# A transformer block's matrix products: high parts first, low parts last, with a new order in the opening and in the up stage

## The chip, the cores and the metric

The kernel runs on one core of a Trainium2 chip. The metric is the device time of one execution in microseconds (us). Three executions of the kernel before took 2151.69, 2151.9 and 2154.22 us; the median is 2151.9. Besides TensorE (PE), the core has VectorE (DVE), ScalarE (ACT), GpSimd (POOL) and SyncE (SP); the last one here issues most transfers.

## The reference

One residual block on a sequence of 2048 tokens of 1024 channels, float32:

```python
h = rmsnorm(x, norm_mix_pre)
u_pool, u_glu, g_a, g_b = split(h @ w_in)          # 512, 1024, 1024, 1024 columns
branch_a = pool_mixer(u_pool, ...)                 # trailing means, group maps, projection
branch_b = conformer_conv(u_glu, ...)              # GLU, causal conv of width 31, LayerNorm, swish, projection
merged = sigmoid(g_a) * branch_a + sigmoid(g_b) * branch_b
x = x + rmsnorm(merged @ w_o, norm_mix_post)
h = rmsnorm(x, norm_mlp_pre)
f = square(relu(h @ w_up)) @ w_down                # 1024 -> 4096 -> 1024
x = x + rmsnorm(f, norm_mlp_post)
```

## The kernel before

**Parts.** Every factor is kept as a high part in the type fp32r (`wh` of a weight, `big` or `tr` of a cell; a cast on ACT, line 237 for weights and 230 in the opening) and a low part (`wl`, or `big` and `tr` again; the rest, a subtraction on DVE at line 131). A product adds three of the four partial products: high by high, weight's high by cell's low, weight's low by cell's high.

**Products.** The large matrix products are cut in blocks of 1024 by 1024 tokens or channels and computed by schemes that need seven block products for eight (`Octet`, with its numbered products 1 to 7, `sink` receiving the finished blocks). Such a block product works on two cells of two 128-row pieces each (k = 0 to 3) and two output halves (q = 0, 1): 2 x 4 x 3 = 24 matmuls of 128x128 by 128x512. `product()` (line 301) issues them with `matmuls()` (line 276) for one half after the other, in the order of `passes()` (line 271): for each k high by high and then weight's high by cell's low, and the weight's low part last, just ahead of the last k. So a cell's low part is used from the second matmul on, the second cell's from the sixth, the weight's low part from the seventh. `in_order()` (line 312) issues them by a table of (q, k, weight part, cell part) and can call a function ahead of the n-th (`inside`). While the kernel is in its opening, `product()` uses the table STAIRS (line 59): cell by cell high by high, cell's low, weight's low, each for both halves.

**Stages.** The program runs, for two batches of 1024 tokens, the input projection (glu, pool, ga, gb), branch A, the merge with branch B (`B`), the output projection, and the up and down stages. The up stage of the first batch, 8 octets (`mlp_up(0, parts)`, line 1897), runs while the second batch's convolution is still to be done on DVE: 31 steps for each of four channel groups (lines 1066 and 1070), and then its norm over the channels (`norm_steps`, whose last parts are at lines 1133 to 1143). These steps are handed out by a lane with a rate, the number of steps per product; `conv1.rate` is 1.2 (line 1854), and `faster()` sets it to 2.8 after a given product of the second octet (`then(faster, octs[1])`, line 1898). Then B of the second batch begins. The norm ends for each of the four pieces so: load of the convolution `yd` to `tr`, times the factor `r` (DVE), sigmoid and gain (ACT), product of the two (DVE), store to `zd`, load of `zd` to `big`, cast at line 1205 (ACT), low part (DVE). B's matmuls take these `big` cells.

**What sets the order.** Every engine works through its own queue in the order of the program as a scheduler has laid it out; an instruction under `tc.high_priority(offset=URGENT)` is put further ahead. SP's queue holds loads and stores in one order, and an entry that waits holds back those behind it. In the up stage `sink` (line 1568) adds a held partial sum to the finished sum in PSUM (`mark(add(o, ps, s))`, line 1571, DVE line 128), which frees the PSUM buffer for a later product.

**The opening.** Lines 1690 to 1757 write out by hand the first eight block products (the glu's) with the loading, norming and splitting of the tokens' cells: `first_gain` (a gain on ACT), `first_cell` (line 924, times the norm factor on DVE), `cells0` (the split), `parts.need` (differences of cells), `n1.spread()` (the norm factor of the second 512 tokens, by eight small matmuls, and its copy to `r` on ACT).

Of the kernel before, what the change touches and what calls it, by code (L numbers as in the profile page):

```python
# [32 lines left out]
URGENT = 1500  # L33
# [22 lines left out]
START = ((0, 1), (0, 2), (1, 2), (1, 1), (0, 5), (0, 6), (0, 3), (0, 7))  # L56
START += ((1, 6), (0, 4), (1, 5), (1, 7), (1, 3), (1, 4))
ORDER = (1, 2, 6, 5, 7, 3, 4)
STAIRS = tuple(
    (q, 2 * c + k, wp, xp)  # L60
    for c in (0, 1) for wp, xp in ((0, 0), (0, 1), (1, 0)) for q in (0, 1) for k in (0, 1)
)
COMING = tuple((q, k, 0, 0) for k in (0, 1) for q in (0, 1)) + ((0, 0, 0, 1), (1, 0, 0, 1))
COMING += ((0, 2, 0, 0), (1, 2, 0, 0), (0, 0, 1, 0), (0, 1, 1, 0), (0, 2, 1, 0), (0, 3, 0, 0))
COMING += ((1, 3, 0, 0), (0, 3, 1, 0), (0, 1, 0, 1), (1, 1, 0, 1)) + tuple((1, k, 1, 0) for k in range(4))
# [11 lines left out]
def block_kernel(  # L77
# [14 lines left out]
    nc = tc.nc  # L92
# [34 lines left out]
    def add(o, a, b):  # L127
        return nc.vector.tensor_tensor(o, a, b, op=ALU.add)  # L128
# [21 lines left out]
    def mark(i):  # L150
        marks[i.ins.engine] = i.ins
        return i
# [145 lines left out]
            tuple(part[:, c * T : (c + 1) * T] for part in cell) for cell in cells for c in (0, 1)  # L298
        ]

    def product(ps, w, cells, start=True, stop=True):

        if in_opening:
            in_order(STAIRS, ps, w, cells, start, stop)
            return
        rhs = cell_rhs(cells)
        i = [matmuls(half_of(ps, q), w, 4 * q, rhs, start, stop) for q in (0, 1)]
        mark(i[1])

    in_opening = [True]  # L310

    def in_order(order, ps, w, cells, start, stop, inside=(None, None)):

# [147 lines left out]
    class Octet:  # L461
# [16 lines left out]
        def prepare(self, i):  # L478
            self.w[i] = self.weight(i)

        def run(self, i, then, bg):
            w, cells = self.w.pop(i, None) or self.weight(i), self.parts.need(i)
            if then is not None:
                self.parts.need(then)
            acc = {1: "x", 2: "z", 6: "x", 5: "y", 7: "x", 3: "y", 4: "x"}[i]
            begins = i in (1, 5) or (i == 2 and not self.seeded)
            if begins:
                self.ps[acc] = psum(self.lab)
            ps = self.ps[acc]
            product(ps, w, cells, start=begins, stop=i in (2, 3, 4))  # L490
            flush()
            if i == 1 and self.seeded:
                self.ps["z"] = psum(self.lab)
                mark(nc.scalar.copy(self.ps["z"], ps))
            elif i == 2 and self.seeded:
                self.sink(0, 0, ps, None)
            elif i == 1:
                self.s1 = self.held(ps)
                if self.s2 is not None:
                    self.sink(0, 0, self.s2, self.s1)  # L500
            elif i == 2 and self.s1 is None:
                self.s2 = self.held(ps)
            elif i == 2:
                self.sink(0, 0, ps, self.s1)
            elif i == 6:
# [13 lines left out]
    class Plain:  # L519
# [57 lines left out]
        def run(self, job, then, bg, inside=(None, None)):  # L577
            m, t, k = job
            w = self.w.pop(job, None) or self.weight(*job)
            cells = self.parts.need(self.part(job))  # L580
            if then is not None:
                self.parts.need(then)
            if k == 0:
                self.ps = psum(self.lab)
            if t == 0:
                order = COMING if (m, k) == (0, 0) else STAIRS
                in_order(order, self.ps, w, cells, k == 0, k == 1, inside)
            else:
                product(self.ps, w, cells, start=k == 0, stop=k == 1)
            flush()  # L590
            bg()
            if k and t:
                self.sink(m, t, self.ps, None)
            elif k:
                self.block[m] = tr()
                mark(nc.scalar.copy(self.block[m], self.ps))
# [326 lines left out]

    def first_cell(c, t):
        x = x0[c, t]
        if t or c > 1:
            first_gain(c, t)
            mul(two(x), two(x), per_token(r0[t]))
            return x
        for i in (0, 1):  # L930
            s = slice(i * T, (i + 1) * T)
            nc.vector.scalar_tensor_tensor(
                x[:, s], x[:, s], col(C_PRE + 2 * c + i), r0[t], op0=ALU.mult, op1=ALU.mult
            )
        return x
# [618 lines left out]
    def mlp_up(b, parts):  # L1554
        def one(u):
            f, other = {}, {}
            late = (b and u >= 2) or u >= 4

            def fetch_other():
                h = u - SLABS  # L1560
                for k, at in (
                    (("T3", (1, h, (0, 0))), ("T2", (1, h, "T1")), ("T4", (0, u, (0, 0))))
                    if u >= SLABS else (("T1", (0, u, (0, 0))),)
                ):
                    other[k] = fo()
                    load(other[k], fd[at])

            def sink(m, t, ps, s):
                o = tr()
                if s is not None:  # L1570
                    mark(add(o, ps, s))
                    ps = o
                mark(nc.scalar.activation(o, ps, AF.Relu))
                nc.scalar.activation(o, o, AF.Square)
                f[m, t] = o

                def keep(i, cell, how=load):
# [12 lines left out]
                if len(f) == 3 and (1, 0) not in f:  # L1590
                    d = tr()
                    sub(d, f[1, 1], f[0, 1])
                    keep("t3", d)
                    if late:
                        sub(f[0, 1], f[0, 1], f[0, 0])
                        keep("t1", f[0, 1])
                    if late:
                        e = f["e"] = tr()
                        add(e, d, f[0, 0])
                        keep("t2", e)  # L1600
                if late and (m, t) == (1, 0):
# [71 lines left out]
    def opening():  # L1673
# [50 lines left out]
        with tc.high_priority(offset=URGENT):  # L1724
            cells0(2, 0)
            n1.root()
            cells0(3, 0)
            parts.step()
            o2.prepare(2)
            first_gain(0, 1)  # L1730
            parts.need(2)
            first_gain(1, 1)
        fix()
        o2.run(1, None, none)
        with tc.high_priority(offset=URGENT):
            n1.spread()
            o1.prepare(0, 1, 0)
            o1.get(1)
            cells0(0, 1), cells0(1, 1)
            first_gain(2, 1)  # L1740
            parts.need(8)
            first_gain(3, 1)
        fix()
        o2.run(2, None, none)
        with tc.high_priority(offset=URGENT):
            o1.prepare(0, 1, 1)
            cells0(2, 1), cells0(3, 1)
            parts.need(3)
            o1.cast_behind = [
                i for i in nc.cur_bb.bb.instructions if i.engine == mybir.EngineType.Activation  # L1750
            ][-1]
        fix()
        o1.load_behind = fix.last[E.SP]
        dve.last.update(fix.last)
        in_opening.clear()

    opening()
    with behind():
# [136 lines left out]
        conv1.rate = 2.8  # L1895

    octs = mlp_up(0, parts)
    then(faster, octs[1])
    run(octs, soon=3)
    empty()  # L1900
    early.close()
# [569 lines left out]
    for n, (s, i, b) in enumerate(END):  # L2471
        if n == 0:
            acc[0, b] = psum("down")
        end.append(coming.pop(0))
        product(acc[0, b], weight_down(i, s, 0), end[n], start=n == 0, stop=s == LAST)
        if n + 2 < SLABS:
            coming.append(token_cells(*END[n + 2]))
        w = [weight_down(i, n, 1, BIG)] if n == 0 else w + [weight_down(i, n, 1, BIG)]
        if s == LAST:
            last_product(i, 0, b, acc[0, b])  # L2480
        bg()
# [75 lines left out]
```

## Time and profile before

| | |
|---|---|
| median of three executions | 2151.9 us |
| the profiled execution | 2153.48 us |
| its span in the profile | 2151.7 us |
| matmuls on PE | 9549 |
| DVE instructions, busy | 1621, 1653.8 us |
| mean clock granted to PE | 0.997 of full |

The span runs from the first to the last instruction that the profiler recorded; the execution's own time holds 1.78 us more around it. In the rows below, a line gives the start in us, the busy time, the engine, the source line, the operation with its output and inputs, and in brackets how long the engine stood idle before it and which instruction's end released it.

### The profile page before, as it was taken

How to read it: one execution, taken by the hardware profiler on the slowest of the kernel's cores; microseconds unless marked ns; L12 is line 12 of the kernel's file. 1: busy time of each engine (PE TensorE's matmuls, PEld its weight loads, DVE VectorE, ACT ScalarE, POOL GpSimd, SP SyncE). 2: the span in 40 equal slices, each digit the busy share in tenths (PEclk: the TensorE clock that was granted, in tenths of full speed). 3: DMA queues.
4: the chain of work that ended last, by engine and by line, in shares of the span. 5: the costliest groups of instructions: out<-in, count | busy, mean ns of one | idle time of the engine just before them, and what ended most of it. 6: DMA issues, size and time to landing. Idle time of an engine off the chain costs nothing.

```text
span 2151.7 us, 25228 instructions
## 1 busy us (share of the span) xinstructions
PE 2130.3 (99%) x9549; PEld 1764.8 (82%) x9549; DVE 1653.8 (77%) x1621; ACT 1047.7 (49%) x1123; POOL 78.4 (4%) x143
## 2 busy tenths in 40 slices
PE   9999999999999999999999999999999999999998
PEld 7888888888888887888888888888888888888887
DVE  7898589997778869997868795667776657576975
ACT  8445454334443635445554684645663332234751
POOL 1000000000000000000000000000000000120002
PEclk9999999999999999999999999999999999999999
DMA  8789897768897787445697698677898997996977
GB/s 309 250 301 344 310 354 263 270 246 304 338 362 251 267 320 270 169 148 200 248 352 296 244 347 319 249 262 277 316 347 313 346 379 258 336 366 236 302 260 209
DMA packets 174506, 620.49 MB, mean 288 GB/s; under 512 B 19504, under 2 KB 21808, under 8 KB 174384
## 3 DMA queue, kind: packets, MB, share of 16 engines
q1 hardware_dynamic: 143456, 508.01, 64.8%
q0 software_dynamic: 17824, 64.07, 8.4%
q10 hardware_dynamic: 13104, 46.80, 5.5%
q8 instruction: 75, 1.23, 0.2%
q14 instruction: 47, 0.39, 0.0%
HBM read 408.99 MB, written 209.81 MB: 288 GB/s over the span
## 4 chain that ended last, share of the span: by engine, by line
PE 90%; DVE 5%; DMA 3%; ACT 1%; issue 1%; SPq 0%; DVEq 0%; ACTq 0%
PE up L280 24%; PE down L280 22%; PE wo L280 8%; PE ga L280 7%; PE gb L280 7%; PE glu L280 5%; PE rb L280 5%; PE A L280 4%; PE B L280 4%; PE pool L280 3%; DVE y L1070 1%; DVE big L131 1%; DVE tr L131 1%; PE glu L319 1%; DVE wl L131 1%
## 5 line engine op out<-in xcount | busy, mean ns | idle before, releaser
L280 PE MATMUL up<-big,wh 128*128 128x512 f32 x1792 | 481.3, 390 | 5.0 <-DVE tr L128 4.2
L280 PEld LDWEIGHTS up<-big,wh 128*128 128x128 f32 x1792 | 336.4, 188 | 76.2 <-issue 3.9
L237 ACT CAST wh<-wr 128x1024 fp32r<-128x1024 f32 x196 | 205.8, 1051 | 336.2 <-PE up L280 101.8
L1070 DVE SCALAR_TENSOR_TENSOR y<-v,cst,y 128x1024 f32<-128x1024 f32 x240 | 307.5, 1281 | 3.1
L280 PE MATMUL down<-big,wh 128*128 128x512 f32 x872 | 294.9, 389 | 0.0
L237 ACT CAST wh<-ws 128x1024 fp32r<-128x1024 f32 x128 | 134.6, 1052 | 302.3 <-PE up L280 91.6
L280 PE MATMUL up<-big,wl 128*128 128x512 f32 x896 | 277.0, 390 | 0.0
L280 PE MATMUL down<-big,wl 128*128 128x512 f32 x688 | 212.0, 389 | 0.0
L131 DVE TENSOR_TENSOR wl<-ws,wh 128x1024 fp32r<-128x1024 f32 x120 | 146.5, 1221 | 76.1 <-ACT wh L237 75.6
L280 PEld LDWEIGHTS up<-big,wl 128*128 128x128 f32 x896 | 168.7, 188 | 35.0
L280 PE MATMUL down<-tr,wh 128*128 128x512 f32 x504 | 196.2, 389 | 0.5 <-DVE tr L131 0.5
L280 PEld LDWEIGHTS down<-big,wh 128*128 128x128 f32 x872 | 163.6, 188 | 33.9
L131 DVE TENSOR_TENSOR wl<-wr,wh 128x1024 fp32r<-128x1024 f32 (+1 forms) x121 | 146.3, 1211 | 32.3 <-ACT wh L237 32.3
L131 DVE TENSOR_TENSOR big<-big,big 128x1024 fp32r<-128x1024 f32 (+1 forms) x108 | 129.9, 1221 | 41.0 <-ACT big L1205 19.6
L131 DVE TENSOR_TENSOR tr<-tr,big 128x1024 fp32r<-128x1024 f32 x94 | 112.6, 1221 | 56.5 <-ACT big L1975 43.8
L280 PEld LDWEIGHTS down<-big,wl 128*128 128x128 f32 x688 | 129.1, 188 | 26.8
L280 PE MATMUL wo<-big,wh 128*128 128x512 f32 x480 | 128.5, 389 | 0.0
L1975 ACT CAST big<-tr 128x1024 fp32r<-128x1024 f32 x70 | 72.0, 1048 | 102.1 <-DMA tr<-fd 79.9
L280 PE MATMUL gb<-big,wh 128*128 128x512 f32 x448 | 120.1, 389 | 0.0
L280 PE MATMUL ga<-big,wh 128*128 128x512 f32 x448 | 119.8, 389 | 0.0
L280 PEld LDWEIGHTS down<-tr,wh 128*128 128x128 f32 x504 | 94.6, 188 | 20.5 <-DVE tr L131 1.0
L280 PEld LDWEIGHTS wo<-big,wh 128*128 128x128 f32 x480 | 90.0, 188 | 18.5
(248 smaller groups left out, 3427.0 us busy)
## 6 DMA issues: line engine op xcount, KB each, us to landing
tr<-fd SPq DMA_DIRECT2D x98, 512.0 KB, 7.5
wl<-kept SPq DMA_DIRECT2D x85, 512.0 KB, 4.9
wr<-w_down SPq DMA_DIRECT2D x80, 512.0 KB, 7.5
kept<-wl SPq DMA_DIRECT2D x72, 512.0 KB, 6.2
wr<-w_up SPq DMA_DIRECT2D x64, 512.0 KB, 5.3
wr<-w_in SPq DMA_DIRECT2D x59, 512.0 KB, 5.2
fd<-tr ACTq DMA_DIRECT2D x54, 512.0 KB, 5.4
big<-fd SPq DMA_DIRECT2D x48, 512.0 KB, 6.4
```

The source lines that it names most:

```text
L131: return nc.vector.tensor_tensor(o, a, b, op=ALU.subtract)
L237: nc.scalar.copy(hi[:, :n], src[:, :n])
L280: i = nc.tensor.matmul(ps, w[wp][:, (at + k) * P : (at + k + 1) * P], rhs[k][xp], start=start and n == 0, stop=stop and n == len(order) - ...
L319: i = nc.tensor.matmul(half_of(ps, q), w[wp][:, (4 * q + k) * P : (4 * q + k + 1) * P], rhs[k][xp], start=start and q not in seen, stop=st ...
L1070: nc.vector.scalar_tensor_tensor(acc, v[:, k : k + TB], wk, acc, op0=ALU.mult, op1=ALU.add)
L1975: nc.scalar.copy(hi, t)
```

## The change

It has four parts. First, `product()` takes a table: by default LATE_LOWS, which runs the high by high matmuls of both cells first, then the first cell's low part, the weight's low part with both cells, and the second cell's low part last. A cell's low part is used from the 9th matmul on (the first cell's) or from the 21st (the second's), the weight's low part from the 13th. The products at the end of the down stage keep the old order (None); branch A, the merge and the output projection don't go through `product()`. Second, in the opening the fifth and sixth product (`o2.run(1, ...)` and `o2.run(2, ...)`) use STAIRS and issue the work for the second 512 tokens after 20 of their 24 matmuls; cell (3, 1) is normed and gained by two DVE instructions rather than by ACT and DVE; the seventh and eighth product use LOWS_BEHIND. Third, the additions in the up stage's `sink` are put ahead. Fourth, `faster()` is called after a product of the third octet rather than of the second.

```diff
+def cellwise(*steps):
+    return tuple(
+        (q, 2 * c + k, wp, xp) for c, wp, xp in steps for q in (0, 1) for k in (0, 1)
+    )
+STAIRS = cellwise(*((c, *part) for c in (0, 1) for part in ((0, 0), (0, 1), (1, 0))))
+LOWS_BEHIND = cellwise(*((c, *part) for c in (0, 1) for part in ((0, 0), (1, 0), (0, 1))))
+LATE_LOWS = cellwise((0, 0, 0), (1, 0, 0), (0, 0, 1), (0, 1, 0), (1, 1, 0), (1, 0, 1))
...
-    def product(ps, w, cells, start=True, stop=True):
-        if in_opening:
-            in_order(STAIRS, ps, w, cells, start, stop)
+    def product(ps, w, cells, start=True, stop=True, order=LATE_LOWS):
+        if order is not None:
+            in_order(order, ps, w, cells, start, stop)
             return
...
-            product(ps, w, cells, start=begins, stop=i in (2, 3, 4))
+            if inside is not None:
+                in_order(STAIRS, ps, w, cells, begins, i in (2, 3, 4), inside)
+            else:
+                product(ps, w, cells, start=begins, stop=i in (2, 3, 4))
...
-                product(self.ps, w, cells, start=k == 0, stop=k == 1)
+                product(self.ps, w, cells, k == 0, k == 1, LATE_LOWS if m else LOWS_BEHIND)
...
-        if t or c > 1:
+        if (c, t) not in ((0, 0), (1, 0), (3, 1)):
             first_gain(c, t)
             mul(two(x), two(x), per_token(r0[t]))
             return x
...
-                    mark(add(o, ps, s))
+                    with tc.high_priority(offset=URGENT):
+                        mark(add(o, ps, s))
...
-            first_gain(1, 1)
         fix()
-        o2.run(1, None, none)
-        with tc.high_priority(offset=URGENT):
-            n1.spread()
-            o1.prepare(0, 1, 0)
-            o1.get(1)
-            cells0(0, 1), cells0(1, 1)
-            first_gain(2, 1)
-            parts.need(8)
-            first_gain(3, 1)
+        def second_half():
+            with tc.high_priority(offset=URGENT):
+                n1.spread()
+                first_gain(1, 1)
+                o1.prepare(0, 1, 0)
+                o1.get(1)
+                cells0(0, 1), cells0(1, 1)
+                parts.need(8)
+                first_gain(2, 1)
+        def last_cells():
+            with tc.high_priority(offset=URGENT):
+                o1.prepare(0, 1, 1)
+                cells0(2, 1), cells0(3, 1)
+                parts.need(3)
...
+        o2.run(1, None, none, (20, second_half))
         fix()
-        o2.run(2, None, none)
...
+        o2.run(2, None, none, (20, last_cells))
...
-    then(faster, octs[1])
+    then(faster, octs[2])
...
-        product(acc[0, b], weight_down(i, s, 0), end[n], start=n == 0, stop=s == LAST)
+        product(acc[0, b], weight_down(i, s, 0), end[n], n == 0, s == LAST, None)
```

What that moves in the queues is seen in rows of the compiled programs. A row gives the source line, the operation, the output and inputs (tiles with running numbers, which differ by a little between the two programs) and the size. Lines of the changed program are 7 or 8 higher.

The first place is on DVE in the opening, from the norming of the second 512 tokens' last cells on (`big_376` and `big_378` are cells (2, 1) and (3, 1), `r_213` the norm factor). Before:

```order
L134 TENSOR_TENSOR big_372<-big_372,r_213 128x1024
L134 TENSOR_TENSOR big_374<-big_374,r_213 128x1024
L131 TENSOR_TENSOR big_586<-big_372,big_585 128x1024
L131 TENSOR_TENSOR big_590<-big_374,big_589 128x1024
L128 TENSOR_TENSOR tr_621<-glu_595,tr_563 128x1024
L134 TENSOR_TENSOR big_376<-big_376,r_213 128x1024
L134 TENSOR_TENSOR big_378<-big_378,r_213 128x1024
L131 TENSOR_TENSOR tr_648<-big_372,big_217 128x1024
L131 TENSOR_TENSOR big_631<-big_376,big_630 128x1024
L131 TENSOR_TENSOR big_635<-big_378,big_634 128x1024
```
After:

```order
L141 TENSOR_TENSOR big_372<-big_372,r_213 128x1024
L141 TENSOR_TENSOR big_374<-big_374,r_213 128x1024
L138 TENSOR_TENSOR big_578<-big_372,big_577 128x1024
L138 TENSOR_TENSOR big_582<-big_374,big_581 128x1024
L141 TENSOR_TENSOR big_376<-big_376,r_213 128x1024
L940 SCALAR_TENSOR_TENSOR big_378<-big_378,cst,r_213 128x512 x2
L138 TENSOR_TENSOR big_622<-big_376,big_621 128x1024
L138 TENSOR_TENSOR big_626<-big_378,big_625 128x1024
L135 TENSOR_TENSOR tr_634<-glu_593,tr_591 128x1024
L138 TENSOR_TENSOR tr_647<-big_372,big_217 128x1024
L138 TENSOR_TENSOR tr_653<-big_374,big_219 128x1024
```
The cells (2, 1) and (3, 1) now come ahead of the addition `tr_634<-glu_593,...`, their low parts too, and (3, 1) is made by two instructions of line 940.

The second place is on DVE in the first up stage, near the end of an octet (`tr_6615<-up_6287` before and `tr_6614<-up_6286` after are the addition in `sink`; `wl_6672` and `wl_6671` are the low part of a next product's weight, `big_6580` and `big_6586` low parts of cells). Before:

```order
L131 TENSOR_TENSOR tr_6577<-big_5448,tr_6199 128x1024
L1070 SCALAR_TENSOR_TENSOR y_6353<-v_5618,cst,y_6353 128x1024
L131 TENSOR_TENSOR tr_6583<-big_5526,tr_6243 128x1024
L131 TENSOR_TENSOR wl_6672<-wr_6435,wh_6671 128x1024
L131 TENSOR_TENSOR big_6580<-tr_6577,big_6579 128x1024
L131 TENSOR_TENSOR big_6586<-tr_6583,big_6585 128x1024
L128 TENSOR_TENSOR tr_6615<-up_6287,tr_6476 128x1024
L1070 SCALAR_TENSOR_TENSOR y_6353<-v_5618,cst,y_6353 128x1024
```
After:

```order
L138 TENSOR_TENSOR tr_6576<-big_5447,tr_6198 128x1024
L1078 SCALAR_TENSOR_TENSOR y_6352<-v_5617,cst,y_6352 128x1024
L138 TENSOR_TENSOR tr_6582<-big_5525,tr_6242 128x1024
L135 TENSOR_TENSOR tr_6614<-up_6286,tr_6475 128x1024
L138 TENSOR_TENSOR big_6579<-tr_6576,big_6578 128x1024
L138 TENSOR_TENSOR big_6585<-tr_6582,big_6584 128x1024
L138 TENSOR_TENSOR wl_6671<-wr_6434,wh_6670 128x1024
L138 TENSOR_TENSOR tr_6620<-tr_6614,tr_6560 128x1024
L1078 SCALAR_TENSOR_TENSOR y_6352<-v_5617,cst,y_6352 128x1024
```
The addition now stands ahead of the two cells' low parts and the weight's.

The third place is on SP at the end of the first up stage, where the four pieces of the second batch's convolution are loaded (`yd`), stored normed (`zd`) and loaded again, among loads of weights (`wr`, `wl`), stores of the up stage's results (`fd`) and loads for B's merge (`sbd`, `mad`). Before, from the load of the fourth piece:

```order
L137 DMA tr_8370<-yd_168 128x1024
L137 DMA zd_173<-tr_8244 128x1024
L137 DMA zd_174<-tr_8283 128x1024
L137 DMA big_8578<-zd_173 128x1024
L137 DMA zd_175<-tr_8325 128x1024
L137 DMA big_8581<-zd_174 128x1024
L137 DMA zd_176<-tr_8370 128x1024
L137 DMA big_8584<-zd_175 128x1024
L137 DMA wr_8831<-w_co 128x1024
L137 DMA wl_8612<-kept_4937 128x1024
L137 DMA big_8587<-zd_176 128x1024
```
After, from the store that stands ahead of the load of the fourth piece (this program's last rows of the four `zd` stand further down, at the load `big_8586<-zd_176`):

```order
L144 DMA zd_173<-tr_8385 128x1024
L144 DMA wr_8896<-w_o 128x1024
L144 DMA wl_8759<-kept_5094 128x1024
L144 DMA big_8577<-zd_173 128x1024
L144 DMA fd_8507<-tr_8505 128x1024
L144 DMA fd_8510<-tr_8501 128x1024
L144 DMA fd_8514<-tr_8512 128x1024
L144 DMA tr_8516<-yd_168 128x1024
L144 DMA zd_174<-tr_8422 128x1024
L144 DMA wr_8929<-w_o 128x1024
L144 DMA zd_175<-tr_8464 128x1024
L144 DMA big_8580<-zd_174 128x1024
```
The load of the fourth piece (`tr_8516<-yd_168`) now stands behind three stores of the up stage's results; before, all four pieces had been loaded ahead of them. On PE the last matmuls of that norm (`rb`, 4 of line 779 before, 787 after) stand 192 matmuls of the up stage ahead of B's first before, and 96 after.

More of the change, by code (lines that the diff above doesn't have):

```diff
@@ L58 @@
 ORDER = (1, 2, 6, 5, 7, 3, 4)
[L59 to L62, printed above, removed]
+def cellwise(*steps):
[5 more added lines that the diff above has]
+LATE_LOWS = cellwise((0, 0, 0), (1, 0, 0), (0, 0, 1), (0, 1, 0), (1, 1, 0), (1, 0, 1))
 COMING = tuple((q, k, 0, 0) for k in (0, 1) for q in (0, 1)) + ((0, 0, 0, 1), (1, 0, 0, 1))
@@ L308, in product @@
         mark(i[1])
-    in_opening = [True]
     def in_order(order, ps, w, cells, start, stop, inside=(None, None)):
@@ L479, in prepare, with run @@
             self.w[i] = self.weight(i)
-        def run(self, i, then, bg):
+        def run(self, i, then, bg, inside=None):
             w, cells = self.w.pop(i, None) or self.weight(i), self.parts.need(i)
@@ L1731, in opening @@
             parts.need(2)
-            first_gain(1, 1)
         fix()
-        o2.run(1, None, none)
-        with tc.high_priority(offset=URGENT):
-            n1.spread()
-            o1.prepare(0, 1, 0)
-            o1.get(1)
-            cells0(0, 1), cells0(1, 1)
-            first_gain(2, 1)
-            parts.need(8)
-            first_gain(3, 1)
-        fix()
-        o2.run(2, None, none)
[L1745 to L1751, printed above, removed]
+        def second_half():
[12 more added lines that the diff above has]
+                parts.need(3)
+                o1.cast_behind = [
+                    i for i in nc.cur_bb.bb.instructions if i.engine == E.Activation
+                ][-1]
+        o2.run(1, None, none, (20, second_half))
+        fix()
+        o2.run(2, None, none, (20, last_cells))
         fix()
@@ L1754, in opening @@
         dve.last.update(fix.last)
-        in_opening.clear()
     opening()
```

## The prediction

> **What bounds the kernel now.** I read the page first, then the waits of PE, then the timelines of PE, DVE and ACT around the places that the change touches, and last the transfers at the end of the first up stage.
>
> ```profile
> PE 2130.3 (99%) x9549; PEld 1764.8 (82%) x9549; DVE 1653.8 (77%) x1621; ACT 1047.7 (49%) x1123; POOL 78.4 (4%) x143
> ```
> PE is busy for 2130.3 of the span of 2151.7 us. So there are two ways to move the time: the 21 us in which PE stands still, and new waits of PE. DVE, at 77%, limits nothing over the whole, but its queue holds the instructions that PE waits for:
>
> ```profile
> PE up L280 <- DVE tr L128: 4.2, 2, 3.5
> PE glu L280 <- DVE big L131: 1.6, 2, 0.8
> ...
> PE glu L280 <- ACT big L230: 0.9, 1, 0.9
> PE up L280 <- DVE big L131: 0.8, 1, 0.8
> ```
> Each row gives the total, the count and the longest wait in us. The first is the addition of the up stage, the second and third the opening (glu), the fourth a product that begins before its cell's low part is there. All four are touched by the change. A yardstick for the rest is PE's pace in undisturbed stretches:
>
> ```profile
> 1063.12 1.56 PE L280 MATMUL up<-big,wh 128*128 128x512 f32 x6
> ...
> 1106.68 1.52 PE L280 MATMUL B<-big,wh 128*128 128x512 f32 x6
> ...
> 1109.27 0.50 PE L280 MATMUL B<-big,wh 128*128 128x512 f32 x1 [0.16 <-DVE big L131]
> ```
> From 1063.12 to 1106.68 stand 8 products of 24 matmuls, 43.56 us, or 5.44 us a product and 227 ns a matmul. The row at 1109.27 shows that the next stage, B, already waited for its data: there is no slack at this place before the change.
>
> **The additions of the up stage: −6.4 us.** The second wait first, PE above and DVE below:
>
> ```profile
> 841.62 0.39 PE L280 MATMUL up<-big,wl 128*128 128x512 f32 x1
> 845.51 1.83 PE L280 MATMUL up<-big,wh 128*128 128x512 f32 x6 [3.50 <-DVE tr L128]
> ...
> 852.68 1.52 PE L280 MATMUL up<-big,wh 128*128 128x512 f32 x6
> ```
> ```profile
> 840.74 1.22 DVE L131 TENSOR_TENSOR wl<-wr,wh 128x1024 fp32r<-128x1024 f32 x1
> 841.88 2.35 DVE L131 TENSOR_TENSOR big<-tr,big 128x1024 fp32r<-128x1024 f32 x2
> 844.15 1.22 DVE L128 TENSOR_TENSOR tr<-up,tr 128x1024 f32<-128x1024 f32 x1
> ```
> PE should have gone on at 841.62 + 0.23 = 841.85 and went on at 845.51: 3.66 us. The 24 matmuls after it took 852.68 − 845.51 = 7.17 us in place of 5.44, so the stop cost 1.73 us more in slow matmuls. The addition that frees the sum's buffer ran at 844.15, behind three splits; in the new order it stands ahead of those three (3.4 us). It then ends near 842, about when PE asks. The low part of the weight, put behind it, ends near 844; the new product order asks for wl at its 13th matmul, 2.7 us after its start. Both waits go: −5.4.
>
> ```profile
> 806.66 1.23 DVE L128 TENSOR_TENSOR ws<-wr,wr 128x1024 f32<-128x1024 f32 x1 [6.59 <-DMA wr<-w_up]
> 807.80 1.22 DVE L128 TENSOR_TENSOR tr<-up,tr 128x1024 f32<-128x1024 f32 x1
> ```
> ```profile
> 807.94 0.39 PE L280 MATMUL up<-big,wl 128*128 128x512 f32 x1
> 809.08 1.66 PE L280 MATMUL up<-big,wh 128*128 128x512 f32 x6 [0.75 <-DVE tr L128]
> ```
> At the first one DVE sat 6.59 us on a weight with the finished sum behind it. Now the addition stands ahead of that instruction, so it runs in DVE's idle time: −1.0 (809.08 − 807.94 − 0.23, and 0.1 in the slow first matmuls). I take 6.4 together. What it may cost if cover is gone: the weight's splits come one instruction, 1.14 us, later, which the 13th matmul hides. Bounds: 5.4 to 6.4.
>
> **The opening: −2.9 us.**
>
> ```profile
> 42.57 1.07 PE L319 MATMUL glu<-big,wl 128*128 128x512 f32 x4
> ...
> 58.20 1.52 PE L280 MATMUL glu<-big,wh 128*128 128x512 f32 x6
> ```
> The seventh and eighth product begin after the four matmuls at 42.57, at 43.48, and end at 58.20: 14.72 us for 48 matmuls that need 10.88, a loss of 3.84. Now the norm factor of the second tokens comes 4 matmuls (0.9 us) sooner, one gain leaves ACT for two DVE instructions, and the low parts are asked for at the 9th and 21st matmul rather than the 2nd and 6th. Walking the new queues by the same durations, each hi and low is there before it is asked for; the whole loss goes. But DVE must now get through more before the next products' weights:
>
> ```profile
> 53.62 1.22 DVE L131 TENSOR_TENSOR tr<-big,big 128x1024 f32<-128x1024 f32 x1
> ...
> 64.98 1.22 DVE L128 TENSOR_TENSOR ws<-wr,wr 128x1024 f32<-128x1024 f32 x1
> ```
> From 53.62 to 64.98 DVE ran ten instructions without a gap, 1.14 us each. In the new order it is no sooner at the sum ws, while PE, 3.84 us earlier, would ask for it some 0.9 us before its cast is done. I book −3.84 + 0.95 = −2.9; bounds 0 (DVE is the limit and the same wait stands behind) and −3.8.
>
> **Low parts asked for later: −1.5 us.**
>
> ```profile
> 1263.31 1.29 PE L280 MATMUL up<-big,wh 128*128 128x512 f32 x5
> 1265.39 0.50 PE L280 MATMUL up<-big,wh 128*128 128x512 f32 x1 [0.79 <-DVE big L131]
> ```
> The 6th matmul waited; 15 matmuls (3.4 us) more of cover end that. This row gives 0.79, like ones at other products some 0.7: 1.5. Bounds: 0.8 to 2.3 with their slow restarts. Elsewhere the products take as long as before: each matmul count is the same, and the order costs nothing where the weight loads (82%) lie beside the matmuls, as they do now.
>
> **The faster convolution comes later: +27.6 us.** This is the one line that reads like nothing: the rate of the second batch's convolution steps rises from 1.2 to 2.8 steps a product after the third octet rather than the second. That is 7 products later; 7 × 1.6 = 11.2 steps are missing, at 2.8 a product 4 products. In the new PE order the last matmuls of the second batch's convolution norm stand 4 products ahead of the first matmul of B, where 8 stood (1063.12 to 1106.68). B needs the normed convolution as its right-hand side, and the chain behind the norm does not get shorter by that:
>
> ```profile
> 1087.52 1.23 DVE L134 TENSOR_TENSOR tr<-tr,r 128x1024 f32<-128x1024 f32 x1 [1.11 <-DMA tr<-yd]
> ...
> 1107.99 1.23 DVE L131 TENSOR_TENSOR big<-big,big 128x1024 fp32r<-128x1024 f32 x1 [2.38 <-ACT big L1205]
> ```
> ```profile
> tr<-yd SPq DMA_DIRECT2D x4, 512.0 KB, 6.3
> zd<-tr SPq DMA_DIRECT2D x4, 512.0 KB, 4.3
> big<-zd SPq DMA_DIRECT2D x4, 512.0 KB, 6.0
> ```
> ```profile
> DMA to landing us min/median/max: 3.5/4.8/9.0
> ```
> ```profile
> DMA to landing us min/median/max: 5.5/6.3/7.3
> ```
> The last columns are the landing times; the two last lines are those of zd (stores and loads) and yd. The fourth piece is the last. Counted from the end of the last up product: SP's load of it (yd) stands behind a store that waits for the fifth DVE instruction after the addition of the last but one product, at −5.4 + 6 × 1.14 = +1.4, so it is issued at about 1.9 and lands 6.3 later, 8.2. The product with r, sigmoid, gain and product, on DVE, ACT, ACT, DVE, take some 1.2 us each: 13.0. The store to zd lands at 17.3. The load back is at its worst for the last piece (9.0): 26.3. The cast and the low part, 1.06 and 1.23, end at 28.6. The rows of before agree: from 1087.52 to 1107.99 + 1.23 the same piece took 21.7, and 8.2 + 21.7 = 29.9. B's first product asks for that low part at its 10th matmul, 2.27 us after its start: a wait of 26.3. PE stops for longer than at 841.62, so I add the same 1.73 for slow matmuls, and subtract 0.43 for the waits that B has now: +27.6.
>
> Bounds: with the shortest landings (5.5, 3.5 and 3.5) the low part ends at 19.5, a loss of 18.5; with the longest (7.3, 9.0 and 9.0) at 34.3, a loss of 33.3. Nothing excludes an end below 18.5 but DVE's order: the fourth piece's first product stands behind a subtraction that needs the last up product's square (1.0 + 1.06 + 1.14 after it), so that even with transfers of no length it ends at 10.3, a loss of 9.3.
>
> The POOL queue's transfers of the same size in this window landed in less:
>
> ```profile
> level<-y POOLq DMA_DIRECT2D x1, 512.0 KB, 3.0
> ```
> The Trainium skill, page "DMA: Bandwidth & Descriptors", section "Anatomy of one DMA — SWDGE (gpsimd) path", gives for one transfer of that path 2.0 us and the bytes over 436 GB/s, so 3.2 us for 512 KB as an estimate; this row agrees. By that rule the three transfers here would take 9.6 us and the loss would be 17.6 in place of 27.6, a time near 2159; the SP rows above (6.3, 4.3, 6.0) speak against it, so its chance stays within the main case's range.
>
> **The sum.** Against the profiled execution: 2153.48 − 6.4 − 2.9 − 1.5 + 27.6 = 2170.3. That execution is 1.58 us above the median of 2151.9, so 2168.7, and I say **2169**.
>
> **Rivals.**
> *The gains stand and the tail is hidden (faster).* If the low part of the fourth piece is ready within 2.3 us of the end of the up stage, B doesn't wait, and the time is 2151.9 − 10.8 = 2141. It stays below before's as long as the loss is under 10.8, so as long as that low part is ready 11.8 us after the up stage (a wait of 9.5 and 1.3 of slow matmuls). For it: the landing times of zd spread from 3.5 to 9.0 us, so a better chain than the median exists. Against: the bound of 10.3 without any transfer, and 0.16 us of waiting already at 1109.27. Chance 0.07; another 0.03 for a loss that just cancels the gains.
> *The waits are only passed on.* The additions come sooner, but PE then stops for wl or for the next weight (the 6.59 us that DVE waited for a transfer show how tight weights are), and the opening gains nothing: 2151.9 − 1.5 + 27.6 = 2178. For it: DVE does the same work in the same stretch. Against: PE waits for DVE's order here, not for its load. Chance 0.10.
> *The new order slows PE's pace.* Two neighbours no longer use the same weight, so every matmul needs its own load in time. With 1 ns on some 7,000 matmuls in this order (three quarters of 9549, an estimate) 7 us: 2176. Against it, matmuls in a like order before:
>
> ```profile
> 28.04 1.07 PE L319 MATMUL glu<-big,wl 128*128 128x512 f32 x4
> ...
> 37.11 0.22 PE L771 MATMUL rb<-ident,sp 128*128 128x128 f32 x1
> ```
> The 40 matmuls from 28.04 to 37.11 took 226.8 ns each, no more than the 227 above. Chance 0.05.
>
> **How the numbers follow.** The forecast has 0.75. Its own range is 18.5 to 33.3 for the tail and 8 to 11.8 for the gains: 2159 to 2177. The rivals on the slow side (0.15) lie at 2176 and 2178, so 2159 to 2178 leaves out the cases of no or little tail (0.10) and the rivals' upper ends. Within 0.2% (4.3 us, about what a measurement of this kernel can tell from no change): 0.03; faster 0.07; slower 0.90.
>
> **What would show it.** In the changed kernel's waits of PE a row of over 15 us for B on DVE big, where 0.16 stands; behind it matmuls of over 400 ns. The 3.5 us row for up on DVE tr and the 0.9 us row for glu on ACT big gone; the eighth opening product done near 54.4 in place of 58.2 and a wait of about 1 us near 65. The wait at 1263 gone. If B waits less than 5 us, the tail's chain was shorter than I say and the time falls under 2155. If the row for up stays, the rival of passed-on waits is right.

## The result and the profile after

| | before | changed |
|---|---|---|
| median of four executions | 2151.84 us | 2181.59 us |
| lowest and highest | 2151.69, 2154.22 | 2180.24, 2183.04 |
| ratio, 95% interval | | 1.0136 [1.0118, 1.0153] |
| span of the profile | 2151.7 | 2181.2 |
| matmuls, mean clock granted | 9549, 0.997 | 9549, 0.989 |

The kernel became slower by 29.7 us. The direction was forecast, the size was not: 2169 was predicted, with 2159 to 2178 as the range.

First the page's row of busy times, then PE's waits of the changed kernel (engine, output and line, what it waited for: total us, times, longest).

```profile
PE 2132.6 (98%) x9549; PEld 1767.1 (81%) x9549; DVE 1653.0 (76%) x1622; ACT 1048.4 (48%) x1121; POOL 78.2 (4%) x143
```
```profile
PE B L287 <- ACT big L1213: 30.7, 4, 16.7
PE B L287 <- DVE big L138: 2.1, 4, 0.7
...
PE glu L324 <- ACT wh L244: 1.0, 1, 1.0
```
The four rows of up and glu that the prediction started from are gone. In their place stands B with 32.8 us, and the wait of about 1 us for a weight of glu that the prediction had put near 65 us (PE stands from 65.45 to 66.63). PE's timeline where the up stage ends and B begins:

```profile
1095.51 1.07 PE L324 MATMUL up<-big,wh 128*128 128x512 f32 x4
1113.26 0.80 PE L287 MATMUL B<-big,wh 128*128 128x512 f32 x1 [16.67 <-ACT big L1213]
...
1127.47 0.80 PE L287 MATMUL B<-big,wh 128*128 128x512 f32 x1 [9.02 <-ACT big L1213]
...
1134.89 0.80 PE L287 MATMUL B<-big,wh 128*128 128x512 f32 x1 [4.08 <-ACT big L1213]
...
1141.02 0.99 PE L287 MATMUL B<-big,wh 128*128 128x512 f32 x2
```
The up stage's last four matmuls begin at 1095.51 and end at 1096.42 (4 x 0.227). B began at 1106.68 before: the work up to there became 10.3 us shorter. Then B waits for its cells, one after the other, with single matmuls of 0.80 us between, twice their usual 0.39. From 1096.42 to 1141.02 stand 21 matmuls, which need 4.8 us: **the tail costs 39.8 us**, where 0.4 had been lost before. 39.8 − 0.4 − 10.3 = 29.1, and the spans differ by 29.5.

Why the fourth piece is so late stands in SP's queue (start, busy, what was issued) and in the two DVE instructions between:

```profile
1098.65 1.14 SPq L144 DMA_DIRECT2D tr<-yd  x1
...
1110.31 0.42 SPq L144 DMA_DIRECT2D tr<-sbd  x1
...
1113.95 0.48 SPq L144 DMA_DIRECT2D tr<-sbd  x1
1115.30 0.32 SPq L144 DMA_DIRECT2D big<-zd  x1
1116.54 0.32 SPq L144 DMA_DIRECT2D fd<-tr  x1
1117.80 0.32 SPq L144 DMA_DIRECT2D zd<-tr  x1
...
1128.84 0.32 SPq L144 DMA_DIRECT2D big<-zd  x1
```
```profile
1108.49 1.23 DVE L141 TENSOR_TENSOR tr<-tr,r 128x1024 f32<-128x1024 f32 x1 [5.25 <-DMA tr<-yd]
1112.30 1.23 DVE L141 TENSOR_TENSOR tr<-tr,tr 128x1024 f32<-128x1024 f32 x1 [2.58 <-ACT tr L1146]
...
1134.87 1.23 DVE L138 TENSOR_TENSOR big<-big,big 128x1024 fp32r<-128x1024 f32 x1 [6.20 <-ACT big L1213]
```
The load of the fourth piece is issued at 1098.65 and lands at 1108.49. Its last product ends at 1113.53, but its store leaves SP only at 1117.80, behind seven loads for B's merge (1110.31 to 1113.95), another piece's load and a store. What released it is shown by SP's waits, here for 1117.7 to 1117.9 alone:

```profile
SPq L144 <- DMA tr<-mad: 0.9, 1, 0.9
```
It is the landing of the `mad` load issued at 1110.82, eight entries earlier (7.0 us to landing). The entries at 1115.30, 1116.54 and 1119.09 also left within 0.1 us of the landing of the transfer eight entries ahead of them. So the merge's loads held the store not only by their places in the queue, but because they had not landed. The store takes until 1128.84, when the load back can leave. The low part ends at 1136.10. The view by windows shows how loaded the transfers were (window, its length, PE, PEld, DVE, ACT, POOL busy with counts, then clock, share of the DMA engines busy, GB/s), before and after:

```profile
1080.00:1107.00 27.00, 27.00 (x121) 22.37 (x120) 17.60 (x15) 21.61 (x22) 0.00 (x0) 1.00 0.94 339
```
```profile
1099.00:1129.00 30.00, 4.24 (x6) 1.71 (x7) 8.40 (x7) 8.29 (x8) 0.00 (x0) 0.53 0.98 369
```
```profile
DMA to landing us min/median/max: 4.9/8.1/11.1
```
The last row is that of zd's stores and loads after the change; before it read 3.5/4.8/9.0. From 1099 to 1129, while PE mostly stands still, the DMA engines are 98% busy.

### The profile page after: what moved, and what is told of

Same layout as the page of the kernel before. It is cut to its first block, busy times and chain, and to the rows that moved or that the text cites. A ratio compares the mean times of both kernels' runs of the same rounds, so it can differ in the third digit from the quotient of the medians.

```text
span 2181.2 us, 25133 instructions
## 1 busy us (share of the span) xinstructions
PE 2132.6 (98%) x9549; PEld 1767.1 (81%) x9549; DVE 1653.0 (76%) x1622; ACT 1048.4 (48%) x1121; POOL 78.2 (4%) x143
## 4 chain that ended last, share of the span: by engine, by line
PE 92%; DMA 3%; DVE 1%; ACT 1%; issue 0%; POOL 0%; POOLq 0%; SPq 0%; DVEq 0%; ACTq 0%
PE up L324 27%; PE down L324 21%; PE gb L324 7%; PE ga L324 7%; PE glu L324 5%; PE wo L287 4%; PE A L287 4%; PE rb L324 4%; PE B L287 4%; PE pool L324 3%; PE wo L324 3%; PE down L287 2%; DMA wr<-w_o 1%; PE rb L646 1%; DMA zd<-tr 1%; PE rb L287 0%
## 5 line engine op out<-in xcount | busy, mean ns | idle before, releaser
L324 PE MATMUL up<-big,wh 128*128 128x512 f32 x1792 | 427.4, 390 | 0.5 <-ACT tr L480 0.5
L324 PE MATMUL up<-big,wl 128*128 128x512 f32 x896 | 221.2, 389 | 0.0
L324 PE MATMUL down<-big,wh 128*128 128x512 f32 x840 | 204.7, 389 | 0.0
L324 PE MATMUL down<-big,wl 128*128 128x512 f32 x656 | 162.2, 389 | 0.0
L324 PE MATMUL down<-tr,wh 128*128 128x512 f32 x472 | 126.2, 389 | 0.0
L324 PE MATMUL glu<-big,wh 128*128 128x512 f32 x464 | 113.4, 390 | 2.5 <-DVE wh L576 1.5
L324 PE MATMUL ga<-big,wh 128*128 128x512 f32 x448 | 107.6, 389 | 0.0
L324 PE MATMUL gb<-big,wh 128*128 128x512 f32 x448 | 107.5, 389 | 0.0
L287 PE MATMUL B<-big,wh 128*128 128x512 f32 x256 | 74.3, 409 | 32.7 <-ACT big L1213 30.7
L324 PEld LDWEIGHTS glu<-big,wh 128*128 128x128 f32 x464 | 86.8, 188 | 21.4 <-ACT big L860 1.9
```

The costliest lines, as they stand in the source:

```text
L287: i = nc.tensor.matmul(ps, w[wp][:, (at + k) * P : (at + k + 1) * P], rhs[k][xp], start=start and n == 0, stop=stop and n == len(order) - ...
L324: i = nc.tensor.matmul(half_of(ps, q), w[wp][:, (4 * q + k) * P : (4 * q + k + 1) * P], rhs[k][xp], start=start and q not in seen, stop=st ...
```

## The experiments

The theory after the result: all of the loss is B's wait, because the one line on `faster()` put the norm 4 products later, and the transfers behind it met the merge's loads on SP and in the DMA engines. The rivals were a share of the new product order or of the additions in it, and a chain that is simply long.

**e1: the rate as before.** Everything else of the change stays.

```diff
-    then(faster, octs[2])
+    then(faster, octs[1])
```


> The changed kernel with the faster convolution called after the second octet again, as before. Theory (the whole loss is the wait of B at the end of the first up stage, because the norm comes 4 products later): B's four waits of 30.7 us on ACT big and 2.1 on DVE big go, the gains stay (the first matmul of B stood at 1106.68 before and at 1096.4 after, 10.3 us sooner): about 2141 us. Rival (the new product order or the additions put ahead also slow the tail): 2150 or more, with a wait of B of over 5 us left.

Measured: 2141.74 us, ratio 0.9952 [0.9937, 0.9967]. B no longer waits:

```profile
1095.70 1.07 PE L324 MATMUL up<-big,wh 128*128 128x512 f32 x4
1096.61 1.52 PE L287 MATMUL B<-big,wh 128*128 128x512 f32 x6
```
The up stage's last matmul is followed by B's first at once. One line made the whole loss, and without it the change gains 10 us. This version beats both kernels.

**e2: the rate alone**, the same line in the kernel before.

```diff
-    then(faster, octs[1])
+    then(faster, octs[2])
```


> The kernel before with that one call moved to the third octet. Theory: B waits as in the changed kernel, some 40 us with its slow matmuls, and nothing is gained: 2151.8 + 39.5 = 2191 us. The prediction's own sum: 2151.8 + 27.6 = 2179. Rival (the loss comes from the mixture with the new order, where the additions stand ahead of the norm's steps on DVE): under 2165.

Measured: 2191.61 us, 1.0186 [1.0171, 1.0201]. The waits of B:

```profile
PE B L280 <- ACT big L1205: 30.9, 3, 17.4
```
The tail costs 38.9 us here by the same count. So the loss comes without the new product order and without the additions put ahead.

**e3: the merge's loads behind.** In the changed kernel, the loads of `sbd` and `mad` lose their priority, so that on SP the last store of zd stands ahead of them.

```diff
-            with tc.high_priority(offset=100) if b else nullcontext():
+            with nullcontext():
                 load(sg, sbd[(b, *k)])
                 load(ma, mad[(b, *k)])
```


> The changed kernel with the loads for B's merge (sbd, mad) put behind the norm's last store and load on SP, nothing else moved. Theory A (the norm's last transfers were slow because these loads, 3.6 MB, ran beside them, and its last store left SP late because it stood behind them): the last store of zd is issued about 4 us sooner and lands in some 5 us instead of 11.0; B's last wait ends some 9 us sooner: 2172 us. Theory B (only SP's queue held it): 4 us, 2177. Rival (the transfers are slow whatever stands beside them and the queue cost nothing): 2181 to 2182.

Measured: 2170.8 us, 1.0086 [1.0071, 1.0101], 10.8 less than the changed kernel. The last store and load on SP:

```profile
1114.16 0.32 SPq L144 DMA_DIRECT2D zd<-tr  x1
...
1119.43 0.32 SPq L144 DMA_DIRECT2D big<-zd  x1
```
Counted from the end of the up stage (1096.75 here) the store leaves at 17.4 rather than 21.4, and takes 5.3 us rather than 11.0. So both parts of theory A are there, 4 us of queue and 5.8 of traffic. The tail's cost falls to 28.8. That it comes near the 27.6 of the prediction's sum is luck: the load of the fourth piece takes 10.1 us here, as slow as in the changed kernel (9.8) although no merge load is issued before 1114.53, and the load back takes only 4.3.

The number of transfers under way fits both landing times of the store. At 1117.80 in the changed kernel it was the eighth of eight 512 KB transfers that had not landed, 4.2 MB; at the 369 GB/s of that stretch this gives 11.4 us as an estimate, and 11.0 were measured. In e3 it was the fourth of four, 2.1 MB at 364 GB/s: 5.8 us as an estimate, 5.3 measured.

**e4: the rate sooner**, after the first octet (10 products ahead of B).

```diff
-    then(faster, octs[2])
+    then(faster, octs[0])
```


> The changed kernel with the faster convolution called after the first octet, one sooner than before. Theory: B has all its cells in time, so at most the 0.4 us that it lost before go: 2139 to 2142 us. Rival (7 products with 2.8 steps each crowd DVE, and the additions or weights of the up stage come late): over 2145, with waits of up on DVE or ACT.

Measured: 2147.54 us, 0.9977 [0.9968, 0.9987]. The rival holds:

```profile
PE up L324 <- ACT tr L1582: 4.1, 1, 4.1
```
One wait of the up stage for ACT costs 4.1 us, and the matmuls behind it are slow. So the call can stand too early as well; of the places tried, the old one is best.

**e8, e10 and e9: between.** With `octs[2]` and a product's number the norm stands 6 (e8) or 7 (e10) products ahead of B; e9 is e8 with e3's edit.

```diff
-    then(faster, octs[2])
+    then(faster, octs[2], 6)     # e8, e9; in e10: 1
```


> The changed kernel with the faster convolution called three products after the second octet (rather than seven), which puts the norm's last matmuls 6 products ahead of B (4 in the changed kernel, 8 before). Theory (8 products just cover the chain, each product less costs its own 5.44 us, and a stop of some length also costs slow matmuls): 2141.7 + 10.9 + 1.7 = 2154 us. Rival 1 (the loss sets in only below 6 products): 2142 to 2144. Rival 2 (half of the loss of 39.9 between 4 and 8): 2162.

> The changed kernel with the faster convolution called one product after the second octet, which puts the norm's last matmuls 7 products ahead of B; on SP all stores and loads of zd still stand ahead of the merge loads. Theory (a cliff: what costs is a zd store behind the merge loads; up to there each product less costs at most its 5.44 us): 2143 to 2148 us. Rival (a slope: 40 us over the first two products, so some 20 for one): 2155 or more.

> The kernel of e8 (6 products) with the loads for B's merge behind the norm's transfers on SP, as in e3. Theory (in e8 the fourth piece was done at 1101.8 but its store left SP only at 1116.2, behind six merge loads, and B waited 19.4 us for it): the store leaves near 1102, lands near 1107, the load near 1113, the low part is there near 1115.5 in place of 1136.3; some 20 us less, 2158 to 2163 us. Rival (the store is slow because the chain behind the norm is long, not because of SP's order): 2178 or more.

Measured: e8 2181.88 us, 1.0132 [1.0117, 1.0148]; e10 2159.97, 1.0036 [1.0022, 1.005]; e9 2174.24, 1.01 [1.0085, 1.0116]. None of the three came out as its theory said; e10's rival (2155 or more) did. e8 is as slow as the changed kernel although its norm comes two products sooner. Its tail at B is 8.1 us shorter (table below), but PE now stops earlier, near 1041 for ACT and near 1070 for the norm's own matmuls. With the slow matmuls behind them these stops cost 8.0 us:

```profile
PE up L324 <- ACT tr L480: 2.0, 2, 1.6
PE rb L787 <- DVE tr L755: 1.9, 2, 1.6
```
Its fourth piece on DVE, and SP's queue:

```profile
1100.62 1.22 DVE L141 TENSOR_TENSOR tr<-tr,tr 128x1024 f32<-128x1024 f32 x1
```
```profile
1107.72 1.28 SPq L144 DMA_DIRECT2D tr<-sbd  x1
...
1116.18 0.42 SPq L144 DMA_DIRECT2D zd<-tr  x1
```
The piece is ready at 1101.84 and its store leaves 14.3 us later. Until 1106.72 a weight load and another piece's load back stand ahead of it, then three stores and the six merge loads. In e9 the store leaves as soon as the piece is ready (1099.4), and B's waits fall from 25.4 to 5.4 us, as its theory said (the low part ends at 1114.1). But the time falls by 7.6 only, because the merge's loads are now late themselves:

```profile
PE wo L324 <- DVE big L135: 12.0, 1, 12.0
PE B L287 <- ACT big L1213: 4.0, 3, 3.0
```
The output projection waits 12.0 us for the merged cells, 14.2 with the slow matmuls behind it: most of the 19.8 us that e9 gains at B (table below) is given back there. Another 2.5 us are gained ahead of B. In e10 the tail costs 13.1 us, not the 5.4 of one product. Its fourth store leaves SP late too (1099.39, 5 us after the product), behind another piece's load and loads of weights, and takes 8.5 us:

```profile
1099.39 0.44 SPq L144 DMA_DIRECT2D zd<-tr  x1
...
1107.92 0.32 SPq L144 DMA_DIRECT2D big<-zd  x1
```
The faster steps also fall into another stretch: near 1027 the up stage waits 3.9 us for ACT, at the same line as in e4, 6.5 with slow matmuls. 13.1 + 6.5, less e1's tail of 0.4, are 19.2 us; the two spans differ by 19.3, the medians by 18.2. The tail by place of the norm, counted in each trace like the 39.8 above:

| products ahead of B | kernel | tail, us | median, us |
|---|---|---|---|
| 8 | e1 | 0.4 | 2141.74 |
| 7 | e10 | 13.1 | 2159.97 |
| 6 | e8 | 31.7 | 2181.88 |
| 6 | e9, merge loads behind | 11.9 | 2174.24 |
| 4 | changed | 39.8 | 2181.59 |
| 4 | e3, merge loads behind | 28.8 | 2170.8 |

So the tail is neither a cliff nor a slope of 5.44 a product: the first two products cost 13 and 19 us, the next two 4 each. At 6 products 19.8 of its 31.7 us go with the place of the merge's loads on SP, though the time hardly shows it.

**e5, e6, e7: the gains one by one**, each part of the change alone in the kernel before: the additions with priority; LATE_LOWS for all products outside the opening; the opening.

```diff
+                    with tc.high_priority(offset=URGENT):        # e5
+                        mark(add(o, ps, s))
...
+    def product(ps, w, cells, start=True, stop=True, order=LATE_LOWS):   # e6
...
+        o2.run(1, None, none, (20, second_half))                 # e7, with the opening's other edits
```


> The kernel before with the up stage's additions put ahead, nothing else. Theory: the two waits of up on DVE tr (4.2 us) and the slow matmuls behind them go: 6.4 us less, 2145.3. Rival (the waits are passed on to the weight's low part, which stands behind the addition and is asked for at the 7th matmul in the old order): a wait of up on DVE wl of 1 us or more, 2147 to 2151.

> The kernel before with LATE_LOWS for the products outside the opening, nothing else. Theory: only waits for low parts go, 1.5 us: 2150.2. Rival 1 (the order itself slows the pace, since neighbours no longer use the same weight): 2153 or more. Rival 2 (it helps the additions too): under 2148.

> The kernel before with the opening's edits alone (STAIRS and the work inside the fifth and sixth product, LOWS_BEHIND for the seventh and eighth). Theory: the loss of 3.84 us between 43.5 and 58.2 goes and a wait of about 1 us for the next weight comes near 65: 2.9 us less, 2148.8. Rival (DVE is the limit, the wait moves on whole): 2151 to 2152.

Measured: e5 2149.89 us, 0.9987 [0.9978, 0.9996]; e6 2143.73, 0.9958 [0.9945, 0.997]; e7 2150.3, 0.999 [0.9981, 0.9999]; the kernel before beside them 2152.2. The additions alone bring 2.3 (0.9 to 4.7 by the interval), the order alone 8.5 (6.5 to 11.8), the opening 1.9 (0.2 to 4.1). The prediction had 6.4, 1.5 and 2.9; the interval of the opening doesn't exclude its 2.9. What e5 has left, on DVE and PE:

```profile
808.38 1.23 DVE L128 TENSOR_TENSOR ws<-wr,wr 128x1024 f32<-128x1024 f32 x1 [6.49 <-DMA wr<-w_up]
809.53 1.22 DVE L128 TENSOR_TENSOR tr<-up,tr 128x1024 f32<-128x1024 f32 x1
...
842.46 1.22 DVE L128 TENSOR_TENSOR tr<-up,tr 128x1024 f32<-128x1024 f32 x1
843.59 2.35 DVE L131 TENSOR_TENSOR big<-tr,big 128x1024 fp32r<-128x1024 f32 x2
845.86 1.21 DVE L131 TENSOR_TENSOR wl<-wr,wh 128x1024 fp32r<-128x1024 f32 x1
```
```profile
844.86 1.64 PE L280 MATMUL up<-big,wh 128*128 128x512 f32 x5 [0.57 <-DVE big L131]
847.13 0.96 PE L280 MATMUL up<-big,wl 128*128 128x512 f32 x3 [0.63 <-DVE wl L131]
```
The priority didn't lift the first addition (809.53) over the weight's sum, which waits for its transfer. The second (842.46) came ahead of the three splits, and PE then waited for the cells' and the weight's low parts behind it, the kind of wait that the rival named, though 0.63 us for `wl` and not 1 or more. In e6, without any priority, the first addition does stand ahead of the weight's sum. The second still stands behind the splits, but PE waits 1.6 us for it rather than 3.5:

```profile
800.47 1.23 DVE L134 TENSOR_TENSOR tr<-up,tr 128x1024 f32<-128x1024 f32 x1 [0.96 <-PE up L328]
801.61 0.80 DVE L1075 TENSOR_SCALAR y<-v,cst 128x1024 f32<-128x1024 f32 x1
804.87 1.23 DVE L134 TENSOR_TENSOR ws<-wr,wr 128x1024 f32<-128x1024 f32 x1 [2.46 <-DMA wr<-w_up]
...
836.46 2.36 DVE L137 TENSOR_TENSOR big<-tr,big 128x1024 fp32r<-128x1024 f32 x2
838.73 1.22 DVE L134 TENSOR_TENSOR tr<-up,tr 128x1024 f32<-128x1024 f32 x1
```
So the new order of PE alone also moves DVE's queue. Of the 6.4 us that the prediction counted at these two stops, 4.1 remain in e5, 1.7 in e6 and none in e1: the priority alone takes 2.3, the order alone 4.7.

The three gains add up to 12.7 us, more than the 10 of e1, because they overlap. They do so at these stops, and also in the opening: the seventh and eighth product run in LATE_LOWS in e6 and take 13.3 us there, where they took 14.7 before. In e7 they take 10.9, the 48 matmuls' own time.

**e11 and e12: what the additions add to the order.** e11 is e1 without the additions' priority; e12 is e1 once more beside it.

```diff
-                    with tc.high_priority(offset=URGENT):
-                        mark(add(o, ps, s))
+                    mark(add(o, ps, s))
```


> The kernel of e1 without the additions put ahead (so: new order and opening, convolution as before). Theory (with the new order the additions put ahead are worth only the one wait that e6 has left, 1.6 us and its slow first matmuls): 2141.7 + 1.7 = 2143.4 us, with one wait of up on DVE tr of 1 to 2 us. Rival 1 (the new order alone covers them): 2141 to 2142, no such wait. Rival 2 (they are worth the predicted 6.4): 2148.

> The kernel of e1 once more, beside e11 on the same chip. Theory: 2141 to 2143 us, 1.7 us under e11. Rival: within 0.5 us of e11, so that the additions put ahead are worth nothing that can be measured.

Measured: e11 2143.22 us (2142.74 to 2146.2), e12 2141.98 (2141.15 to 2143.82), the kernel before 2153.14. In e11 one wait of up for an addition is left, of 0.9 us. The difference of 1.2 us is of the size of the theory's 1.7, but the two groups of five overlap, and their intervals against before (0.9942 to 0.9967 and 0.9936 to 0.9963) do too: it is not settled whether the additions' priority is worth anything on top of the order. That on top of the order it isn't worth 6.4 is settled.

## Why the prediction was wrong, and where it was right

**Right: the change's cause of loss.** The move of `faster()` by one octet was singled out as the part that costs; e1 and e2 show it from both sides.

**Right in sum, wrong in its parts: the gains.** B's first matmul came due 10.3 us sooner, and e1 gains 9.7 to 11.2 us; the sum was 10.8. But 6.4 us were put down to the additions and 1.5 to the product order, and e5 and e6 show 2.3 and 8.5. The step that failed is the attribution in "in the new order it stands ahead of those three". That holds for the changed program, whose rows were those of both edits together, and the text gave their effect to the edit that names the additions. At the first stop the priority alone moves nothing; the product order does. At the second each alone takes more than half.

The opening went as forecast. The eighth product ended at 54.57 us (forecast 54.4, before 58.20), and the new wait, put at 0.95 us near 65, has 1.02:

```profile
66.63 3.06 PE L324 MATMUL glu<-big,wh 128*128 128x512 f32 x12 [1.02 <-ACT wh L244]
```

**Wrong: the size of the tail**, +27.6 where 39.8 − 0.4 = 39.4 came. The step that failed is the chain of the fourth piece. Its terms, from the end of the up stage:

| step | forecast, us | measured, us |
|---|---|---|
| load of yd issued | 1.9 | 2.2 |
| it lands | 6.3 | 9.8 |
| product, sigmoid, gain, product | 4.8 | 5.0 |
| the store waits in SP's queue | 0 | 4.3 |
| the store to zd lands | 4.3 | 11.0 |
| the load back lands | 9.0 | 5.0 |
| cast and low part | 2.3 | 2.3 |
| sum | 28.6 | 39.7 |

The store's wait in SP's queue was not in the sum at all: the rows of the order shown ahead of the prediction end with `big_8580<-zd_174`, and the seven merge loads that stand between it and the fourth store come right after them. The landing times were taken from a stretch of the kernel before in which the chain ran ahead of the merge's loads. For the store that was the error: it took 11.0 us beside those loads, and 5.3 in e3 without most of them. The load of the fourth piece (9.8 us) is another matter, since it landed before the first merge load was issued and is as slow in e3. When it was issued, five other transfers were under way, three of them the stores of the up stage's results that the order shown ahead had placed before it; what they cost it was not tested.

One term was too long: the load back was booked at its worst, 9.0, and took 5.0. That hid 4.0 us of the error by luck. The slow matmuls cost 39.8 − (39.7 − 2.27) = 2.4 us where 1.73 were booked.

The bounds failed too. The upper one, 33.3, took the longest landings of that stretch (7.3 and 9.0), which the load and the store exceeded, and had no term for the queue. The lower one was added up wrongly: the shortest landings give a low part at 21.5 us and a loss of 20.5, not 19.5 and 18.5.

The Trainium skill, page "DMA: Bandwidth & Descriptors", section "Anatomy of one DMA — SWDGE (gpsimd) path", would have had the three transfers at 9.6 us as an estimate by its 2.0 us and 436 GB/s. They took 9.8 + 11.0 + 5.0 = 25.8 on SP's queue: here the measurement decides, and the page's figure, which is for the gpsimd path, was further off than the rows of before.

**Not confirmed: the rivals.** The pace isn't touched by the new order: in e6 24 matmuls of the up stage still take 5.44 us (804.80 to 810.24). The case that the tail is hidden did not come. Waits passed on did occur, with the additions alone (e5) and as the 1 us that was forecast in the opening.

## What to carry to other kernels

When a step that ends in a store and a load back is moved later, write down the whole stretch of the issuing queue up to its last transfer: prefetches with a fixed priority don't move along, and a chain that used to run ahead of them falls behind them. Landing times measured while a chain was early are no bounds for the same chain when it is late: here a store that had landed in 3.5 to 5.5 us took 11.0, with seven other transfers under way. And test each edit of a change apart before its gain is put down to it; here a change that gains 10 us carried one line that loses 40.

## What the runs showed of the hardware that was not expected

A 512 KB store of 4.3 us (median of zd's stores before) took 11.0 us with the DMA engines 98% busy at 369 GB/s, though the engines had been 94% busy at 339 GB/s in the stretch with the 4.3. The busy share doesn't tell the two apart, as e3 shows, where the store took 5.3 us in this stretch:

```profile
1099.00:1126.00 27.00, 6.84 (x10) 2.88 (x10) 9.51 (x8) 9.67 (x10) 0.00 (x0) 0.56 0.97 364
```
What differed was the number of transfers under way, eight and four.

Single matmuls between waits ran at half pace for long: the clock granted from 1099 to 1129 was 0.53, and full pace came back some 6 us after the last wait, which had ended at 1136.15. That time is not fixed: it was 3.4 us in e3 and 4.8 in e10.
